# Sixteen blocks instead of ten in the chunked first stage of a retention trunk block, and branch projections with the tokens stationary

## The chip, the cores and the metric

The kernel runs on one core of a Trainium2 chip. The metric is the device time of one execution in microseconds, median of several runs, lower is better. All data is float32. To keep float32 accuracy a matrix product is made of three products of rounded parts: each operand is split into a rounded part ("hi") and the rest ("lo"), and hi·hi, hi·lo and lo·hi are summed.

## The reference, cut to what matters

```python
D_MODEL = 2048; SEQ = 256; RET_HEADS = 8; RET_HEAD_DIM = 256; D_FF = 5632
mod = silu(c) @ w_ada + b_ada                  # 6 vectors of 2048: sh1, sc1, g1, sh2, sc2, g2
xn = rmsnorm(h) * norm1_g * (1 + sc1) + sh1
proj = xn @ w_in                               # 2048 x 18432
q, k, v, g_ret, bg, cg, xc, gate_logits = split(proj)
y_ret = retention(rotary(q), rotary(k), v)     # 8 heads, in 2 chunks of 128 tokens
y_ret = (y_ret * silu(g_ret)) @ w_ret_o
y_conv = (bg * causal_dwconv(cg * xc, w_sc)) @ w_conv_o
gate_a, gate_b = sigmoid(gate_logits + b_gate)
h = h + g1 * ((gate_a * y_ret + gate_b * y_conv) @ w_mix_o)
...
h = h + g2 * (conv_ffn(modulated rmsnorm(h)) )  # w_gate, w_up: 2048 x 5632, w_down
return rmsnorm(h) * final_g
```

## The kernel before, in words

There are 256 tokens, so every weight matrix is streamed once from device memory, 450 MB in all. The work is a list of **units**. A unit is one piece of weights of 256 rows by 512 columns (512 KB). Its `load` (line 288) puts it into a `raw` tile, of which there are six; its `prep` (line 293) has ScalarE write the rounded part (`hi`, line 300) and VectorE the rest (`lo`, line 301); its `run` does the products on TensorE. A loop at line 1023 goes over the list: at step i it calls the load of unit i+9, the preps up to i+4 (first stage) or i+2, and the run of unit i. A tile framework then gives each engine its order of instructions; it may move an instruction forward when a buffer for it is free. SyncE's queue issues all weight loads in one order, and a load waits there until its `raw` slot is free.

Two forms of a unit's products exist. With the **weights stationary** (`w_block`, line 393, result transposed: channels on partitions) a unit is 8 products of 512 columns (hi weights against hi and lo tokens side by side, line 405) and 8 of 256 columns (line 410). With the **tokens stationary** (`x_block` and `start_block`, lines 376 and 454, through `products`, line 367; result has tokens on partitions) a unit is 12 products of 512 columns.

The vector `mod` has its own units (`Ada`, line 306). VectorE multiplies rows of `w_ada` by a scalar and adds them up (lines 335 and 337), and when 2048 rows are through, TensorE turns the sums into columns with a product with ones (`columns_of`, line 351). The stages of the list are:

- **First stage.** xn needs sh1 and sc1, so it becomes ready in chunks of its 16 tiles of 128 channels, `CHUNKS`: 2, 4, 4, 4, 2 tiles. The `Ada` units of chunk n+1 are spread (`spread`, line 539) between the weight units of chunk n, except for the last `TAILS[n+1]` of them. Ten blocks of 512 columns take part: four of v, four of the swish gate, both with the tokens stationary (`start_block`), and q and k of the first pair of heads (`start_turned`, line 498, 24 products of 256 columns a unit). Each block's partial sum of a chunk is copied (chunk 0, ScalarE) or added (later chunks, VectorE, line 465) to a tile; one block (`IN_PSUM`) stays in its accumulator. That makes 80 units.
- **Heads.** q and k of the other three pairs (48 units, weights stationary), rotary, scores, mixing (`retention`). The decay table is loaded once, 1 MB.
- **Branch A.** For each of four column blocks a merge-gate block (`gate_block`, 8 units) and a block of `w_ret_o` (`ret_block`, 8 units), weights stationary: 64 units.
- **Convolution.** 96 units, weights stationary.
- **Branch B.** For each of four column blocks a merge-gate block and a block of `w_conv_o`: 64 units, weights stationary.
- **Mix** (`w_mix_o`, 32 units, tokens stationary), norm, and the gated MLP (176 units with weights stationary, 88 with tokens stationary).

The other 128 `Ada` units (sh2, sc2, g1, g2) are spread over the stages by `ADA_QK, ADA_RET, ADA_CONV, ADA_OUT` = 8, 28, 42, 32, and the rest, 18, over the first 24 units of the mix.

Of the kernel before, what the change touches and what calls it, by code (L numbers as in the profile page):

```python
# [17 lines left out]
P = 128  # L18
# [20 lines left out]
DEFER_SG, DEFER_ROT = (6, 14, 30, 44), 4  # L39
ROT_EARLY = 12  # L40
ADA_QK, ADA_RET, ADA_CONV, ADA_OUT = 8, 28, 42, 32
# [5 lines left out]
def tile_trunk_block(  # L47
# [8 lines left out]
    w_ada, b_ada, w_in, b_gate, w_sc = w_ada[0], b_ada, w_in[0], b_gate[0], w_sc[0]  # L56
# [146 lines left out]
    vec2 = columns([b_gate, w_sc[0], w_sc[1], w_sc[2]], "vec2")  # L203
# [10 lines left out]
    bgate, wsc = vt2[:, 0:32], vt2[:, 32:80]  # L214
# [67 lines left out]
    class Weights:  # L282
        in_big = False

        def __init__(self, w, r0, c0, run):
            self.w, self.r0, self.c0, self.run_ = w, r0, c0, run

        def load(self):
            self.raw = wpool.tile([P, UK, CB], F32, tag="raw", bufs=6, name=nm("raw"))
            src = self.w[self.r0:self.r0 + UK * P, self.c0:self.c0 + CB]  # L290
            nc.sync.dma_start(self.raw, src.rearrange("(k p) n -> p k n", p=P))

        def prep(self):
# [73 lines left out]
    def products(ps, u, xt, k0, t, first, end):  # L367
        for k in range(UK):
# [62 lines left out]
    def xn1_ready(k0, k1):  # L431
        def done(acc):
# [20 lines left out]

    def start_block(j, in_psum):

        dst = [(v_tok, sg_tok)[j // 4][t][:, (j % 4) * CB:(j % 4 + 1) * CB] for t in range(2)]
        st = {}

        def finish(t, ps, n):
            d = dst[t]  # L460
            if n == 0 and not in_psum:
                nc.scalar.copy(d, ps)
                return
            if not in_psum:
                nc.vector.tensor_tensor(d, ps, d, op=ALU.add)
            if n < len(chunks) - 1:
                return
            if j < 4:
                if in_psum:
                    nc.scalar.copy(d, ps)  # L470
            elif in_psum:
                nc.scalar.activation(d, ps, AF.Sigmoid)
                nc.vector.tensor_tensor(d, d, ps, op=ALU.mult)
            else:
                after(DEFER_SG[j - 4], lambda: swish(d))
# [6 lines left out]
        def run_at(n, k0):  # L482
            def run(u):
# [3 lines left out]
                for t in range(2):  # L487
                    ps = st["ps"][t]
                    products(ps, u, xn1_at, k0, t, c0, c1)
                    if k0 + UK == chunks[n][1] and (not in_psum or k0 + UK == KT):  # L490
# [3 lines left out]
        col = (2 + j // 4) * D + (j % 4) * CB  # L494
        return [[Weights(w_in, k0 * P, col, run_at(n, k0)) for k0 in range(*ch, UK)]
                for n, ch in enumerate(chunks)]

    def start_turned(col, done):

        st = {}  # L500

        def run_at(n, k0):
            def run(u):
                c0, c1 = chunks[n]
                if k0 == c0:
                    st["ps"] = [acc_bank() for _ in range(2)]
                if k0 == 0:
                    st["sum"] = w4("sum", [P, 4, S])
                for i in range(4):
                    ps = st["ps"][i // 2][:, (i % 2) * S:(i % 2 + 1) * S]  # L510
                    for k in range(UK):
                        xk = xn1_at(k0 + k)
                        wh, wl = (w[:, k, i * P:(i + 1) * P] for w in (u.hi, u.lo))

                        first = k0 + k == c0 and i % 2 == 0
                        last = k0 + k == c1 - 1 and i % 2 == 1
                        nc.tensor.matmul(ps, lhsT=wh, rhs=xk[:, 0, :], start=first, stop=False)  # L517
                        nc.tensor.matmul(ps, lhsT=wh, rhs=xk[:, 1, :], start=False, stop=False)  # L518
                        nc.tensor.matmul(ps, lhsT=wl, rhs=xk[:, 0, :], start=False, stop=last)  # L519
                    if k0 + UK == c1 and i % 2:  # L520
                        d = st["sum"][:, i - 1:i + 1, :].rearrange("p k s -> p (k s)")
                        if n == 0:
                            nc.scalar.copy(d, st["ps"][i // 2])
                        else:
                            nc.vector.tensor_tensor(d, st["ps"][i // 2], d, op=ALU.add)
                if k0 + UK == KT:
                    after(DEFER_ROT, lambda: done(st["sum"]))
            return run

        return [[Weights(w_in, k0 * P, col, run_at(n, k0)) for k0 in range(*ch, UK)]  # L530
                for n, ch in enumerate(chunks)]
# [26 lines left out]
    for i, u in enumerate([u for u in units if isinstance(u, Weights)]):  # L558
        u.in_big = i % IN_BIG[1] < IN_BIG[0]
# [57 lines left out]
    dec = {}  # L617
# [27 lines left out]
    def retention(pair, st):  # L645

        def scores():
            st["pt"] = []
            for h2 in range(2):
# [15 lines left out]
        def mix():  # L665
            ss = small.tile([P, 4], F32, tag="ss", name=nm("ss"))
            yp = []
            for h2 in range(2):
                pt, hd = st["pt"][h2], 2 * pair + h2
                cols = slice(hd * S, (hd + 1) * S)  # L670
                ps = misc_bank()
                nc.tensor.matmul(ps[:, 0:S], lhsT=pt[:, 0:P], rhs=v_tok[0][:, cols], start=True, stop=True)
                nc.tensor.matmul(ps[:, S:2 * S], lhsT=pt[:, P:S], rhs=v_tok[0][:, cols], start=True, stop=False)
                nc.tensor.matmul(ps[:, S:2 * S], lhsT=pt[:, S:S + P], rhs=v_tok[1][:, cols], start=False, stop=True)
# [5 lines left out]
            for h2 in range(2):  # L680
                hd = 2 * pair + h2
                for t in range(2):
# [3 lines left out]
                        sg_tok[t][:, hd * S:(hd + 1) * S], op0=ALU.mult, op1=ALU.mult,  # L686
# [21 lines left out]
    def load_decay():  # L708
        dec["t"] = blk8("decay", [P, H, S], F32)
# [360 lines left out]
```

## Time and profile before

| | |
|---|---|
| median of 3 runs | 1921.25 us (1920.57 to 1922.83) |
| the profiled execution's own time | 1922.16 us |
| its span, first to last instruction | 1920.3 us |
| TensorE busy | 1872.8 us, 98% |
| VectorE busy | 1366.4 us, 71% |
| ScalarE busy | 904.9 us, 47% |
| read from device memory | 447.03 MB, mean 234 GB/s over the span |

A matmul that is shown as 0.39 us long overlaps with the next one; what counts is the distance from one start to the next. "Idle before" and the name behind the arrow in a row are the wait ahead of the instruction and the operation that ended it.

### The profile page before, as it was taken

The numbers are of one execution on the slowest core, as the hardware profiler recorded it, in microseconds if no ns is written. First come the engines' busy times: TensorE is split into PE (matmuls) and PEld (weight loads), VectorE is DVE, ScalarE is ACT, GpSimd is POOL, SyncE is SP. The second block draws the span as 40 slices with busy tenths as digits, with TensorE's granted clock in tenths as the row PEclk, the third lists the DMA queues.
The fourth block names the chain that finished last, engine by engine and source line by source line (L and its number), as shares of the span: only waits on it lengthen the run. The fifth ranks groups of instructions, "written<-read, shape, count | busy, mean of one in ns | idle before, by whom it ended". The sixth has DMA issues, their size and how long they took to land.

```text
span 1920.3 us, 26558 instructions
## 1 busy us (share of the span) xinstructions
PE 1872.8 (98%) x10151; PEld 1609.6 (84%) x10151; DVE 1366.4 (71%) x1690; ACT 904.9 (47%) x1187; POOL 22.4 (1%) x52
## 2 busy tenths in 40 slices
PE   4999999999999999999999999999999999999998
PEld 3788888888888888888888787888888888888886
DVE  6889987776676777778777786666665456666655
ACT  3544444444444444444445445555554335555543
POOL 1000000000000000000000000000000000000000
PEclk9899999999999999999999999999999999999999
DMA  8989865666878788787888994666665666666653
GB/s 302 322 305 333 290 218 191 192 199 210 271 267 270 260 271 262 255 283 261 272 274 290 315 318 154 186 187 185 194 192 189 195 190 194 187 189 192 209 195 124
DMA packets 220288, 450.88 MB, mean 235 GB/s; under 512 B 14516, under 2 KB 23040, under 8 KB 219648
## 3 DMA queue, kind: packets, MB, share of 16 engines
q1 hardware_dynamic: 218784, 445.84, 70.8%
q10 hardware_dynamic: 864, 3.15, 0.4%
q8 instruction: 79, 1.29, 0.3%
q14 instruction: 49, 0.40, 0.1%
q0 software_dynamic: 512, 0.20, 0.0%
HBM read 447.03 MB, written 2.10 MB: 234 GB/s over the span
## 4 chain that ended last, share of the span: by engine, by line
PE 90%; DVE 4%; DMA 3%; issue 2%; ACT 1%; POOL 0%; SPq 0%; POOLq 0%; DVEq 0%; ACTq 0%
PE acc L405 42%; PE acc L410 21%; PE acc L373 8%; PE acc L374 8%; PE acc L372 8%; DMA raw<-in_w_ada 2%; DVE lo L301 1%; DVE ada L337 1%; PE misc L351 1%; PE acc L519 1%; PE acc L517 1%; PE acc L518 1%; DVE hl L301 0%; PE misc L247 0%; PE misc L653 0%
## 5 line engine op out<-in xcount | busy, mean ns | idle before, releaser
L300 ACT CAST hi<-raw 128x1024 fp32r<-128x1024 f32 x616 | 647.9, 1052 | 831.9 <-PE acc L405 537.6
L301 DVE TENSOR_TENSOR lo<-raw,hi 128x1024 fp32r<-128x1024 f32 x616 | 748.4, 1221 | 354.3 <-ACT hi L300 351.1
L405 PE MATMUL acc<-xn,hi 128*128 128x512 f32 x3072 | 968.6, 397 | 2.9 <-DVE xn L894 1.8
L410 PEld LDWEIGHTS acc<-xn,lo 128*128 128x128 f32 x3072 | 577.8, 188 | 136.6 <-DVE lo L301 0.2
L410 PE MATMUL acc<-xn,lo 128*128 128x256 f32 x3072 | 605.0, 278 | 0.0
L405 PEld LDWEIGHTS acc<-xn,hi 128*128 128x128 f32 x3072 | 468.8, 189 | 5.2 <-DVE xn L894 2.2
L337 DVE SCALAR_TENSOR_TENSOR ada<-raw,c_act,ada 128x1024 f32<-128x1024 f32 (+1 forms) x199 | 238.8, 1200 | 128.0 <-DMA raw<-in_w_ada 127.0
L372 PE MATMUL acc<-hi,ff_t 128*128 128x512 f32 x332 | 129.2, 389 | 0.0
L373 PE MATMUL acc<-lo,ff_t 128*128 128x512 f32 x332 | 129.2, 389 | 0.0
L374 PE MATMUL acc<-hi,ff_t 128*128 128x512 f32 x332 | 129.1, 389 | 0.0
L416 ACT COPY sb<-acc 128x256 f32<-128x256 f32 x224 | 82.5, 368 | 44.9 <-PE acc L410 37.7
L405 PE MATMUL acc<-y_t,hi 128*128 128x512 f32 x256 | 80.5, 396 | 0.0
L405 PE MATMUL acc<-conv_t,hi 128*128 128x512 f32 x256 | 80.4, 395 | 0.0
L374 PEld LDWEIGHTS acc<-hi,ff_t 128*128 128x128 f32 x332 | 62.3, 188 | 13.0
L372 PEld LDWEIGHTS acc<-hi,ff_t 128*128 128x128 f32 x332 | 62.3, 188 | 13.0
L373 PEld LDWEIGHTS acc<-lo,ff_t 128*128 128x128 f32 x332 | 62.3, 188 | 12.7
L373 PE MATMUL acc<-lo,xn 128*128 128x512 f32 x172 | 69.0, 401 | 1.6 <-DVE lo L301 1.5
L372 PE MATMUL acc<-hi,xn 128*128 128x512 f32 x172 | 68.0, 403 | 2.0 <-ACT hi L300 2.0
L374 PE MATMUL acc<-hi,xn 128*128 128x512 f32 x172 | 68.4, 398 | 0.0
L410 PEld LDWEIGHTS acc<-y_t,lo 128*128 128x128 f32 x256 | 47.9, 188 | 13.7 <-DVE lo L301 2.5
L410 PEld LDWEIGHTS acc<-conv_t,lo 128*128 128x128 f32 x256 | 48.0, 188 | 12.9 <-DVE lo L301 1.6
L410 PE MATMUL acc<-y_t,lo 128*128 128x256 f32 x256 | 50.5, 279 | 1.8 <-DVE lo L301 1.8
(204 smaller groups left out, 1619.4 us busy)
## 6 DMA issues: line engine op xcount, KB each, us to landing
raw<-in_w_in SPq DMA_DIRECT2D x288, 512.0 KB, 4.8
raw<-in_w_ada SPq DMA_DIRECT2D x176, 512.0 KB, 4.8
raw<-in_w_gate SPq DMA_DIRECT2D x88, 512.0 KB, 4.4
raw<-in_w_up SPq DMA_DIRECT2D x88, 512.0 KB, 4.4
raw<-in_w_down SPq DMA_DIRECT2D x88, 512.0 KB, 4.4
raw<-in_w_ret_o SPq DMA_DIRECT2D x32, 512.0 KB, 4.7
raw<-in_w_conv_o SPq DMA_DIRECT2D x32, 512.0 KB, 5.4
raw<-in_w_mix_o SPq DMA_DIRECT2D x32, 512.0 KB, 5.6
```

Of the source, the lines that this page charges most:

```text
L300: nc.scalar.copy(self.hi, self.raw)
L301: nc.vector.tensor_tensor(self.lo, self.raw, self.hi.bitcast(F32), op=ALU.subtract)
L337: nc.vector.scalar_tensor_tensor(acc, self.raw[:, k], c_act[:, kt:kt + 1], acc, op0=ALU.mult, op1=ALU.add)
L351: nc.tensor.matmul(ps[:, i:i + 1], lhsT=flat[:, (s0 + i) * P:(s0 + i + 1) * P], rhs=ones[:, 0:1], start=True, stop=True,)
L372: nc.tensor.matmul(ps, lhsT=xh, rhs=u.hi[:, k, :], start=k0 + k == first, stop=False)
L373: nc.tensor.matmul(ps, lhsT=xh, rhs=u.lo[:, k, :], start=False, stop=False)
L374: nc.tensor.matmul(ps, lhsT=xl, rhs=u.hi[:, k, :], start=False, stop=k0 + k == end - 1)
L405: nc.tensor.matmul(ps, lhsT=u.hi[:, k, i * P:(i + 1) * P], rhs=xt(k0 + k).rearrange("p h s -> p (h s)"), start=k0 + k == 0, stop=False,)
L410: nc.tensor.matmul(ps[:, 0:S], lhsT=u.lo[:, k, i * P:(i + 1) * P], rhs=xt(k0 + k)[:, 0, :], start=False, stop=last and k == UK - 1,)
L416: nc.scalar.copy(b, ps[:, S:2 * S])
L517: nc.tensor.matmul(ps, lhsT=wh, rhs=xk[:, 0, :], start=first, stop=False)
L518: nc.tensor.matmul(ps, lhsT=wh, rhs=xk[:, 1, :], start=False, stop=False)
```

## The change

The first stage sums sixteen blocks instead of ten: v, the swish gate and both merge gates (`start_block`, four blocks each), all with the tokens stationary: 128 units' worth of weights. Chunks are now 2, 3, 3, 4, 4 tiles; in a chunk of three tiles a block has one unit of 512 KB and one of half that size (256 KB, `Weights(..., nk)`), and a load of `w_ada` is 384 KB. q and k of the first pair move to the heads' stage, with the weights stationary. The merge gates stay in SBUF as sums; the bias b_gate is loaded broadcast over the partitions (`gate_of`, a `Loaded` unit), added by VectorE, and the sigmoid follows on ScalarE. The decay table is loaded in four parts, one per pair of heads, by the same class. Both kinds of load use the tag `xtmp`, with two buffers.

`ret_block` and `conv_o_block` become `x_block`s: 64 units go from weights stationary to tokens stationary, and the merged result, which now has tokens on partitions, is transposed by TensorE (`turn_mixed`: 8 transposes per column block, 32 in all). The order of the later stages is: heads (q and k of all four pairs, and the first convolution block), branch A (`w_ret_o` alone, 32 units), the rest of the convolution (88 units), branch B (`w_conv_o` alone, 32 units), mix.

```diff
-IN_PSUM = (4,)
-TAILS = (0, 6, 3, 4, 6)
-CHUNKS = [(0, 2), (2, 6), (6, 10), (10, 14), (14, 16)]
-IN_BIG = (1, 3)
+IN_PSUM = (0,)
+TAILS = (0, 3, 4, 4, 4)
+CHUNKS = [(0, 2), (2, 5), (5, 8), (8, 12), (12, 16)]
+IN_WORK = (1, 3)
...
-ADA_QK, ADA_RET, ADA_CONV, ADA_OUT = 8, 28, 42, 32
+ADA_QK, ADA_RET, ADA_CONV, ADA_OUT = 16, 20, 52, 20
...
     class Weights:
...
         def prep(self):
             if self.in_big:
...
+            elif self.in_work:
+                self.hi, self.lo = (
+                    work.tile([P, self.nk, CB], F32R, tag="w4", name=nm(n)) for n in ("hw", "lw"))
...
+    def parts(k0, k1):
+        return [(k, min(UK, k1 - k)) for k in range(k0, k1, UK)]
...
-        dst = [(v_tok, sg_tok)[j // 4][t][:, (j % 4) * CB:(j % 4 + 1) * CB] for t in range(2)]
+        q, c = j // 4, j % 4
+        if q < 2:
+            dst = [(v_tok, sg_tok)[q][c // 2][:, c % 2, t, :] for t in range(2)]
+        else:
+            dst = [(gate_a, gate_b)[q - 2][t][:, c * CB:(c + 1) * CB] for t in range(2)]
...
-    blocks = [start_block(j, j in IN_PSUM) for j in range(8)]
-    ret0 = {}
-    for key in "qk":
-        col = 0 if key == "q" else D
-        blocks.append(start_turned(col, (lambda key: lambda x: rotate(x, ret0, key))(key)))
+    blocks = [start_block(j, j in IN_PSUM) for j in range(16)]
...
+    class Loaded(Call):
...
+        def load(self):
+            self.t = work.tile(self.shape, F32, tag="xtmp", bufs=2, name=nm("ld"))
+            nc.sync.dma_start(self.t, self.src)
...
+    def gate_of(gate, m, j):
+
+        def prep():
+            for t in range(2):
+                g = gate[t][:, j * CB:(j + 1) * CB]
+                nc.vector.tensor_tensor(g, g, got.t, op=ALU.add)
+                nc.scalar.activation(g, g, AF.Sigmoid)
+        c0 = m * D + j * CB
+        got = Loaded(b_gate[0:1, c0:c0 + CB].to_broadcast([P, CB]), [P, CB], prep)
+        return got
+
+    def ret_block(j):
+        cols = slice(j * CB, (j + 1) * CB)
+
+        def e(t, ps):
+            g = gate_a[t][:, cols]
+            nc.vector.tensor_tensor(g, ps, g, op=ALU.mult)
+        return x_block(w_ret_o, 0, j * CB, lambda kt: y_t[kt // 4][:, kt % 4], KT, e)
...
+    def turn_mixed(j):
+        mb = blk8("mixed", [P, 4, 2, S], F32R)
+        mixed.append(mb)
+        for g in range(2):
+            ps = misc_bank()
+            for k in range(2):
+                c0 = (4 * j + 2 * g + k) * P
+                for t in range(2):
+                    nc.tensor.transpose(
+                        ps[:, k * S + t * P:k * S + (t + 1) * P], gate_a[t][:, c0:c0 + P], ident)
+            split(ps.rearrange("p (k s) -> p k s", k=2), mb[:, 2 * g:2 * g + 2])
+
+    def conv_o_block(j):
+        cols = slice(j * CB, (j + 1) * CB)
+
+        def e(t, ps):
+            a, b = gate_a[t][:, cols], gate_b[t][:, cols]
+            nc.vector.tensor_tensor(b, ps, b, op=ALU.mult)
+            nc.vector.tensor_tensor(a, a, b, op=ALU.add)
+            if t == 1:
+                after(2, lambda: turn_mixed(j))
+        return x_block(w_conv_o, 0, j * CB, lambda kt: conv_t[kt // 4][:, kt % 4], KT, e)
```

How this moves instructions shows at three places. In the following rows a name's number is that of its tile; `lo`, `lw` and `hl` are remainders of weights, `ada` the running sum of `w_ada`, `raw` a landed load.

**Chunk 0 on VectorE** (lines 301 and 337 before, 305 and 341 now). Before:

```order
L301 TENSOR_TENSOR lo_335<-raw_299,hi_334 128x1024
L337 SCALAR_TENSOR_TENSOR ada_269<-raw_304,c_act,ada_269 128x1024
L337 SCALAR_TENSOR_TENSOR ada_269<-raw_307,c_act,ada_269 128x1024
L337 SCALAR_TENSOR_TENSOR ada_269<-raw_310,c_act,ada_269 128x1024
L337 SCALAR_TENSOR_TENSOR ada_269<-raw_313,c_act,ada_269 128x1024
L301 TENSOR_TENSOR lo_369<-raw_332,hi_368 128x1024
```

Now:

```order
L305 TENSOR_TENSOR lw_317<-raw_282,hw_316 128x1024
L341 SCALAR_TENSOR_TENSOR ada_272<-raw_286,c_act,ada_272 128x768
L305 TENSOR_TENSOR lo_340<-raw_302,hi_339 128x1024
L341 SCALAR_TENSOR_TENSOR ada_272<-raw_308,c_act,ada_272 128x768
L305 TENSOR_TENSOR lw_349<-raw_311,hw_348 128x1024
```

Four steps of the sum of `w_ada` stood between two units of weights; now there is one, three quarters as wide, and the sixteen steps are spread over thirteen units instead of four.

**One block of chunk 2 on VectorE** (adds are line 465 before, 479 now). Before:

```order
L465 TENSOR_TENSOR v_tok_226<-acc_1147,v_tok_226 128x512
L465 TENSOR_TENSOR v_tok_227<-acc_1148,v_tok_227 128x512
L337 SCALAR_TENSOR_TENSOR ada_968<-raw_1080,c_act,ada_968 128x1024
L301 TENSOR_TENSOR lo_1189<-raw_1112,hi_1188 128x1024
L337 SCALAR_TENSOR_TENSOR ada_968<-raw_1141,c_act,ada_968 128x1024
L301 TENSOR_TENSOR lo_1212<-raw_1161,hi_1211 128x1024
```

Now:

```order
L479 TENSOR_TENSOR v_tok_226<-acc_1433,v_tok_226 128x512
L479 TENSOR_TENSOR v_tok_226<-acc_1434,v_tok_226 128x512
L305 TENSOR_TENSOR lo_1484<-raw_1421,hi_1483 128x512
L305 TENSOR_TENSOR lw_1498<-raw_1427,hw_1497 128x1024
L341 SCALAR_TENSOR_TENSOR ada_1234<-raw_1447,c_act,ada_1234 128x1024
```

A block of chunk 2 was two units of weights and two steps of `ada`; it is now a unit, half a unit and one step, with the same two adds.

**The gate biases, in the heads' stage** (third and fourth pair). SyncE's queue now:

```order
L327 DMA raw_4806<-in_w_ada 128x1024
L681 DMA ld_5301<-in_b_gate 128x512
L292 DMA raw_4828<-in_w_in 128x2x512
L292 DMA raw_4850<-in_w_in 128x2x512
L681 DMA ld_5527<-in_b_gate 128x512
L292 DMA raw_4884<-in_w_in 128x2x512
L681 DMA ld_5696<-in_b_gate 128x512
```

VectorE now:

```order
L305 TENSOR_TENSOR lo_4809<-raw_4607,hi_4808 128x1024
L341 SCALAR_TENSOR_TENSOR ada_3186<-raw_4806,c_act,ada_3186 128x1024
L693 TENSOR_TENSOR gate_a_229<-gate_a_229,ld_5301 128x512
L221 TENSOR_SCALAR r_y_4798<-ss_4781 128x4
L693 TENSOR_TENSOR gate_a_230<-gate_a_230,ld_5301 128x512
L647 SCALAR_TENSOR_TENSOR y_tok_4801<-misc_4782,r_y_4798,sg_tok_228 128x256 x2
L647 SCALAR_TENSOR_TENSOR y_tok_4801<-misc_4790,r_y_4798,sg_tok_228 128x256 x2
L305 TENSOR_TENSOR lo_4831<-raw_4629,hi_4830 128x1024
L693 TENSOR_TENSOR gate_a_229<-gate_a_229,ld_5527 128x512
L693 TENSOR_TENSOR gate_a_230<-gate_a_230,ld_5527 128x512
L305 TENSOR_TENSOR lo_4887<-raw_4692,hi_4886 128x1024
L693 TENSOR_TENSOR gate_a_229<-gate_a_229,ld_5696 128x512
```

VectorE at the same place before, where no gate stood:

```order
L301 TENSOR_TENSOR lo_3490<-raw_3282,hi_3489 128x1024
L301 TENSOR_TENSOR lo_3512<-raw_3304,hi_3511 128x1024
L337 SCALAR_TENSOR_TENSOR ada_2202<-raw_3437,c_act,ada_2202 128x1024
L221 TENSOR_SCALAR r_y_3479<-ss_3462 128x4
L683 SCALAR_TENSOR_TENSOR y_tok_3482<-misc_3463,r_y_3479,sg_tok_228 128x256
```

All eight loads of b_gate, those of branch B included, were moved forward by the framework into the last pairs of heads. Each stands on SyncE's queue between loads of weights, and VectorE's adds of it stand between the remainders of weights. The loads take turns in one of the two `xtmp` buffers, since the fourth pair's decay keeps the other one until its scores are done.

## Rows read from the trace of the kernel before

**Rows 1.** The page: TensorE's busy time, and its granted clock in 40 slices.
```profile
PE 1872.8 (98%) x10151; PEld 1609.6 (84%) x10151; DVE 1366.4 (71%) x1690; ACT 904.9 (47%) x1187; POOL 22.4 (1%) x52
...
PEclk9899999999999999999999999999999999999999
```
**Rows 2.** Timeline of TensorE, weights stationary: start us, us, instruction, count.
```profile
414.61 0.62 PE L405 MATMUL acc<-xn,hi 128*128 128x512 f32 x2
...
439.69 0.63 PE L405 MATMUL acc<-xn,hi 128*128 128x512 f32 x2
```
**Rows 3.** The same timeline, tokens stationary (last down-projection).
```profile
1802.00 0.40 PE L372 MATMUL acc<-hi,ff_t 128*128 128x512 f32 x1
...
1813.11 0.39 PE L373 MATMUL acc<-lo,ff_t 128*128 128x512 f32 x1
```
**Rows 4.** Stretches: us, busy us of PE, PEld, DVE, ACT, POOL, PEclk, DMA share, GB/s.
```profile
32.26:67.11 34.85, 26.64 (x80) 18.65 (x81) 28.54 (x30) 14.57 (x21) 0.00 (x0) 0.71 0.89 312
67.11:280.50 213.39, 212.29 (x1134) 183.51 (x1133) 193.18 (x236) 96.55 (x111) 0.00 (x0) 1.00 0.87 296
...
280.50:437.00 156.50, 156.22 (x898) 136.51 (x897) 117.56 (x149) 69.42 (x105) 3.04 (x3) 1.00 0.60 192
```
**Rows 5.** Timeline of TensorE in chunk 0, waits in brackets.
```profile
32.26 0.93 PE L372 MATMUL acc<-hl,xn 128*128 128x512 f32 x2 [3.29 <-ACT hl L300]
...
39.75 0.50 PE L373 MATMUL acc<-lo,xn 128*128 128x512 f32 x1
...
44.33 0.73 PE L372 MATMUL acc<-hi,xn 128*128 128x512 f32 x2 [2.02 <-ACT hi L300]
...
51.86 0.73 PE L372 MATMUL acc<-hl,xn 128*128 128x512 f32 x2 [1.68 <-ACT hl L300]
...
58.37 2.12 PE L351 MATMUL misc<-ones,ada 128*128 128x1 f32 x16 [1.12 <-DVE ada L337]
...
67.11 0.63 PE L372 MATMUL acc<-hi,xn 128*128 128x512 f32 x2
```
**Rows 6.** Timeline of VectorE in chunk 0.
```profile
45.91 5.24 DVE L337 SCALAR_TENSOR_TENSOR ada<-raw,c_act,ada 128x1024 f32<-128x1024 f32 x4
```
**Rows 7.** Chain of waits: the column products of chunk 2's sums.
```profile
123.39 1.68 PE misc L351 x16
```
**Rows 8.** Timeline of VectorE in chunk 2.
```profile
144.03 1.28 DVE L465 TENSOR_TENSOR v_tok<-acc,v_tok 128x512 f32<-128x512 f32 x2
145.23 1.27 DVE L337 SCALAR_TENSOR_TENSOR ada<-raw,c_act,ada 128x1024 f32<-128x1024 f32 x1
146.43 1.21 DVE L301 TENSOR_TENSOR lo<-raw,hi 128x1024 fp32r<-128x1024 f32 x1
147.56 1.27 DVE L337 SCALAR_TENSOR_TENSOR ada<-raw,c_act,ada 128x1024 f32<-128x1024 f32 x1
```
**Rows 9.** Groups by line: `ada` steps of half width, and the rounding of weights.
```profile
L337 DVE SCALAR_TENSOR_TENSOR ada<-raw,c_act,ada 128x512 f32<-128x512 f32 x30 | 22.4, 745 | 0.3
...
L300 ACT CAST hi<-raw 128x1024 fp32r<-128x1024 f32 x616 | 647.9, 1052 | 831.9 <-PE acc L405 537.6 <-PE acc L374 181.0 <-issue 38.0
```
**Rows 10.** Loads issued from 72 to 230 us: count, KB, median us to landing.
```profile
raw<-in_w_in SPq DMA_DIRECT2D x57, 512.0 KB, 5.0
...
raw<-in_w_ada SPq DMA_DIRECT2D x16, 256.0 KB, 4.4
```
**Rows 11.** The page's DMA issues: reloads of x during the mix.
```profile
h_tok<-in_x SPq DMA_DIRECT2D x8, 256.0 KB, 7.0
```
**Rows 12.** Waits of SyncE's queue, 72 to 280 us: total us, times, longest.
```profile
SPq L291 <- DVE lo L301: 60.4, 36, 4.9
```
**Rows 13.** Timeline of VectorE at the start of branch A.
```profile
475.71 1.28 DVE L337 SCALAR_TENSOR_TENSOR ada<-raw,c_act,ada 128x1024 f32<-128x1024 f32 x1 [5.47 <-DMA raw<-in_w_ada]
```
**Rows 14.** Waits of TensorE after 280.5 us: total us, times, longest.
```profile
PE acc L410 <- DVE lo L301: 3.0, 2, 1.8
```
**Rows 15.** Timeline of TensorE: eight transposes of 128 columns.
```profile
1175.08 1.04 PE L847 MATMUL misc<-ident,h_tok 128*128 128x128 f32 x8
```

More of the change, by code (lines that the diff above doesn't have):

```diff
@@ L367, in products @@
     def products(ps, u, xt, k0, t, first, end):
-        for k in range(UK):
+        for k in range(u.nk):
             xk = xt(k0 + k)
@@ L460, in finish @@
             d = dst[t]
-            if n == 0 and not in_psum:
+            if in_psum or n == 0:
                 nc.scalar.copy(d, ps)
-                return
-            if not in_psum:
+            else:
                 nc.vector.tensor_tensor(d, ps, d, op=ALU.add)
[L466 to L475, printed above, removed]
+            if n == len(chunks) - 1 and q == 1:
+                after(DEFER_SG, lambda: swish(d))
         def swish(d):
@@ L489, in run @@
                     products(ps, u, xn1_at, k0, t, c0, c1)
-                    if k0 + UK == chunks[n][1] and (not in_psum or k0 + UK == KT):
+                    if k0 + nk == c1:
                         finish(t, ps, n)
             return run
-        col = (2 + j // 4) * D + (j % 4) * CB
-        return [[Weights(w_in, k0 * P, col, run_at(n, k0)) for k0 in range(*ch, UK)]
+        col = (2, 3, 7, 8)[q] * D + c * CB
+        return [[Weights(w_in, k0 * P, col, run_at(n, k0, nk), nk) for k0, nk in parts(*ch)]
@@ L496, in start_block @@
                 for n, ch in enumerate(chunks)]
[L498 to L531, printed above, removed]
@@ L706, in retention @@
         return st
-    def load_decay():
-        dec["t"] = blk8("decay", [P, H, S], F32)
-        tc.keep_in_program_order(nc.scalar.dma_start(dec["t"], decay))
-    units.insert(len(units) - 8, Call(load_decay))
-    seq = []
-    for pair in range(4):
-        st = retention(pair, ret0 if pair == 0 else {})
-        if pair > 0:
-            seq += rot_block(pair * CB, st, "q")
-            seq += rot_block(D + pair * CB, st, "k")
-    units += spread(seq, take(ada_mid, ADA_QK))
-    def gate_block(col, store, key):
-        def e(i, a, b):
-            if i == 0:
-                store[key] = w4("gate", [P, 4, S])
-            nc.vector.tensor_tensor(b, a, b, op=ALU.add)
-            t = (col - 7 * D) // P + i
-            nc.scalar.activation(store[key][:, i, :], b, AF.Sigmoid, bias=bgate[:, t:t + 1])
-        return in_block(col, e)
@@ L749, in tile_trunk_block, with __init__, decay_of @@
-    units += spread(seq, take(ada_mid, ADA_RET))
+    class Loaded(Call):
+        def __init__(self, src, shape, prep=None):
+            super().__init__(prep=prep)
+            self.src, self.shape = src, shape
+        def load(self):
+            self.t = work.tile(self.shape, F32, tag="xtmp", bufs=2, name=nm("ld"))
+            nc.sync.dma_start(self.t, self.src)
+    def decay_of(pair, st):
+        got = Loaded(decay[:, 2 * pair:2 * pair + 2, :], [P, 2, S], lambda: st.update(dec=got.t))
+        return got
@@ L783, in e_b @@
                 split(st["y"], yb)
-        return (in_block(5 * D + j * CB, e_c) + in_block(6 * D + j * CB, e_x)
-                + in_block(4 * D + j * CB, e_b))
+        return [in_block(5 * D + j * CB, e_c), in_block(6 * D + j * CB, e_x),
+                in_block(4 * D + j * CB, e_b)]
+    convs = [b for j in range(4) for b in conv_blocks(j)]
+    seq = []
+    for pair in range(4):
+        st = retention(pair, {})
+        seq += rot_block(pair * CB, st, "q")
+        seq.append(decay_of(pair, st))
+        seq += rot_block(D + pair * CB, st, "k")
```

100 lines of the change are left out of this document (40 added, 60 removed).

## The prediction, made before the changed kernel was run

> **What bounds the kernel now.** I read the page first. TensorE is busy 98% of the span [rows 1], but its instructions overlap, so I went to the timeline for the distance from start to start. With the weights stationary, 36 groups of two 512-column and two 256-column products take 25.08 us [rows 2], 0.697 us each; four groups make a unit, 2.787 us. With the tokens stationary, 49 steps take 11.11 us [rows 3], 0.2267 us each; twelve make a unit, 2.720 us. The list has 448 units of the first form after 280.5 us and 120 of the second: 448 x 2.787 + 120 x 2.720 = 1575.0 of the 1639.8 us that are left there. The other 64.8 us are retention, transposes, broadcasts, the second norm and the tail, which the change leaves. So from 280.5 us on TensorE sets the time, and almost nothing is to be had there except by a cheaper form.
>
> Then I split the first stage [rows 4]. From 67.11 to 280.5 us TensorE runs through: 59 units with tokens stationary are 160.5 us, 48 column products at 0.105 [rows 7] are 5.0, and what is left, 47.9, is at most 2.99 for each of the 16 turned units. From the first weight product at 32.26 to 67.11 us it is different: five units, 13.6 us of work, take 34.85. The rows of TensorE show waits for weights of 2.02 and 1.68 us between units [rows 5], and VectorE shows why: between two units it does four `ada` steps, 5.24 us [rows 6], and the next unit's remainder comes after them. The waits also cost the clock: its mean over this stretch is 0.71 [rows 4], between its two levels of 1.2 and 2.4 GHz. The fourteen products from 32.26 to 39.75 us take 0.53 us each; the ten from there to the wait that ends at 44.33 take 0.26, near the full pace; the twelve after this wait, up to the next one, again 0.49 [rows 5]. The clock rose after TensorE had worked on and fell after it had waited 2 us. About 21 us are lost here, and this is the largest loss that the change can touch.
>
> **The change, part by part.** All sums are against the profiled execution: span 1920.3, time 1922.2, so 1.9 us lie around the span; the median of the runs is 0.9 us below it.
>
> *Chunk 0.* Sixteen units now stand against sixteen `ada` steps of three quarters the width, thirteen of the units mixed with them. Per unit VectorE has one remainder, 1.13 us by its distance to the next instruction, and 16/13 of a step. A step of 384 columns twice is not in the trace; it lies between 0.745 [rows 9] and 1.20 us [rows 8], and I take 0.95, the middle of the two, hence 2.3 us a unit, under TensorE's 2.72. Loads: 0.524 MB and 16/13 of 0.393 MB, 1.01 MB a unit; at the 312 GB/s of this stretch [rows 4], which contains times when the queue had nothing to issue, 3.2 us; over thirteen units that could hold TensorE back by some 2.5 us, and it is part of the waits taken below. At first TensorE is slower than either (5.1 us a unit at the low clock), so a stock of units builds up, it does not wait, and the clock rises as it did at 39.75. Up to there 14 products took 7.49 us instead of 3.17: a loss of 4.3, and the only one that I take. The first product itself stays at 32.26 us: the first chunk of `ada` is as wide as before.
>
> *First stage as a whole.* 32.26 + 4.3 + 128 x 2.720 (348.2) + 56 column products x 0.105 (5.9) = 390.7 us. VectorE must keep up. A block of chunk 2 was two remainders, two adds and two steps, 2 x 1.13 + 1.20 + 2 x 1.20 = 5.86 us [rows 8], against 5.44 of TensorE. A block is now a remainder and half a one (1.13 + 0.60, the half priced as one of the two adds, which have its size), two adds 1.20, one step 0.95 (chunk 1) or 1.20 (chunk 2): 3.88 or 4.13 us against 18 x 0.2267 = 4.08. In chunk 3 it is 1.13 x 2 + 1.20 + 1.20 = 4.66 against 5.44. So VectorE is just enough, with a lead of about one block. I take 3 us of waits; the lower end is 0, the upper 25 (second rival). End of the stage: 393.7.
>
> *The rest.* Of the 448 units, the 64 of the gates went into the first stage and 64 of the branches changed form; the 16 of q and k came in: 336 x 2.787 + 184 x 2.720 = 936.4 + 500.5 us. The branches' change of form alone is 64 x 0.067 = 4.3 us. The Trainium skill (TensorE: Matmul & The Clock Gate, Back-to-back issue gap) gives another price: a gap of N/2.4 + 2.5 ns, by which I estimate 2.59 us for the one form and 2.60 for the other, and the 4.3 us would be nothing; rows 2 and 3, from one execution, differ by 0.067 us, and I go by them. The other work is 64.8 us as before. The 32 added transposes are 0.13 us each by eight in 1.04 [rows 15]: 4.2. Their copies replace the split of the merged result. The four decay loads replace one, and each is issued well before its scores: nothing, unless they queue with the gate biases, which the next part prices.
>
> *The gate biases.* Eight loads of 256 KB pass through one buffer, each issued only after VectorE's adds of the one before, and each holds VectorE, in order, until it lands. Landing is 4.4 us by the nearest row [rows 10], 7.0 in a crowded stretch [rows 11]. By the order of rows VectorE has 1.1 to 8 us of other work between one bias's adds and the next's; for five or six of the eight it is short by 1 to 3 us, about 11 together. The adds are 8 x 1.20 = 9.6. VectorE is idle 39 of 156.5 us in the heads' stage [rows 4], 12 in the 50 us concerned, so it falls behind by 8 to 9. A wait of 5.47 us on VectorE [rows 13] left TensorE no longer wait than 1.8 anywhere later [rows 14]: the stock of two prepared units covers some 5. I take 4; the ends are 0 and 20 (landing 7.0).
>
> *Crowding.* Twenty `ada` steps instead of 18 in the mix, 52 loads in 32 units of branch A and of B: 2 us, from the 1.8 us waits of [rows 14]; the lower end is 0.
>
> Sum: 393.7 + 936.4 + 500.5 + 64.8 + 4.2 + 4 + 2 = 1905.6; with the 1.9 around it 1907.5, against the median 1906.6. I say **1907**. The gain of 14 us is the 17 us of chunk 0's waits and clock, some 9 of cheaper form, less 4 of transposes and 7 to 9 of new waits.
>
> **The rivals.** *Gate biases at full price*: the loads land late behind the weights of the same queue, and VectorE's hold is paid by TensorE: 6 to 16 us on top, 1913 to 1923. For it: eight holds in a row on one buffer; against: landing 4.4 us and the cover above.
>
> *Raw slots* (the one on the slower side): six `raw` slots now carry smaller loads. SyncE's queue does wait for VectorE to free a slot, 36 times for a remainder alone [rows 12]. A block of chunks 1 and 2 needs three loads; at TensorE's pace 4.08 us each slot must turn round in 8.2 us. Landing 5.0, cast 1.05 [rows 9] and remainder 1.13 make 7.2; in [rows 8] a slot turned in 5.86 x 6/4 = 8.8 with VectorE never idle; over all of chunk 1, 39 loads (23 of weights, 16 of `w_ada`) in the 65 us from 58.37 [rows 5] to 123.39 [rows 7], it was 10.0. At 10.0 a block takes 5.0 us, 0.92 more, 29 for the 32 blocks, less a lead of 4: 1929. It decides from about 8.5 us a turn on, where the lead is used up; at 9.5 nothing of the gain is left. The Trainium skill (DMA: Bandwidth & Descriptors, Bandwidth) speaks for it: loads should be batched to a megabyte or more, small ones paying a fixed cost of about 2 us; no row gives that cost, and [rows 10] has 256 KB landing sooner than 512.
>
> *The clock falls again in chunk 0*: three gaps, each 4.3 us: 1920, no change.
>
> *The form is worth nothing*: the distance of 0.2267 us holds where one `raw` unit after the other is ready, and in the branches, beside the `ada` steps, the 128 units that change form stay at 2.787. That is 8.6 us more, 1916. The Trainium skill's gap, above, comes to the same; rows 2 and 3 speak against it.
>
> **How the numbers follow.** A measurement of this kernel can tell a difference of about 0.2%, 3.8 us. Forecast (1900 to 1912) 0.58; everything hidden, all three waits 0 and the clock rising sooner, 1896 to 1899, 0.05; gate biases 0.15, of it 0.08 below 1917.4; raw slots 0.11, of it 0.10 slower; clock 0.08, of it 0.06 no change and 0.02 slower; form 0.03. Faster is 0.58 + 0.05 + 0.08 + 0.03 = 0.74, no change 0.07 + 0.01 + 0.06 = 0.14, slower 0.10 + 0.02 = 0.12. The range goes from 1896 to 1925: it leaves out the upper part of the raw slots.
>
> **What would show it.** Chunk 0 without waits of TensorE over 1 us and a clock mean near 0.9 between 32 and 67 us; the first product of 512 columns with weights stationary at 391 to 397 us; blocks of chunks 1 and 2 at 4.1 to 4.3 us; steps of 0.227 us in branches A and B; the heads' stage with waits for `ld` on VectorE and under 6 us on TensorE. Wrong it is if the first stage ends after 405 us, or if TensorE waits over 10 us in the third and fourth pair of heads.

## The result, and the profile after

The changed kernel is slower: 1947.8 us (median of 4 runs, 1940.5 to 1949.7) against 1921.0 before, a ratio of 1.0131 with a 95% interval of 1.0104 to 1.0157 (four runs of each). The forecast was 1907, its range ended at 1925. The profiled execution took 1947.83 us, its span is 1945.9.

The page of the changed kernel: busy times, and the chain of waits by engine.

```profile
PE 1880.9 (97%) x9543; PEld 1583.9 (81%) x9543; DVE 1385.3 (71%) x1695; ACT 892.2 (46%) x1150; POOL 22.0 (1%) x51
...
PE 75%; DMA 12%; DVE 8%; issue 3%; ACT 1%; POOL 0%; SPq 0%; DVEq 0%; POOLq 0%; ACTq 0%
PE acc L409 26%; PE acc L414 13%; DMA raw<-in_w_ada 12%; PE acc L377 11%; PE acc L376 11%; PE acc L378 11%; DVE lo L305 4%; DVE ada L341 2%; PE misc L355 1%; DMA ld<-in_b_gate 0%; PE misc L247 0%; PE misc L619 0%; ACT hi L304 0%; DVE gate_b L783 0%; DMA raw<-in_w_in 0%
```

Busy shares have hardly moved [rows 1]. New is that 12% of the chain are landings of `w_ada`, which were 2% in the kernel before: TensorE no longer sets the time everywhere. The stages, cut at the first product of each kind on TensorE (first stage, heads, branch A, rest of the convolution, branch B, mix), with the columns of [rows 4]:

```profile
32.26:67.11 34.85, 32.66 (x126) 25.24 (x127) 24.84 (x24) 20.42 (x30) 0.00 (x0) 0.92 0.89 293
67.11:399.60 332.49, 331.69 (x1471) 271.32 (x1470) 285.92 (x358) 152.33 (x184) 0.00 (x0) 1.00 0.81 269
399.60:638.20 238.60, 231.41 (x1314) 200.44 (x1313) 170.71 (x215) 105.84 (x163) 4.41 (x5) 0.99 0.65 205
638.20:736.90 98.70, 92.92 (x403) 74.56 (x402) 65.14 (x63) 34.04 (x33) 0.00 (x0) 0.98 0.80 262
736.90:1000.10 263.20, 255.55 (x1445) 220.35 (x1444) 206.20 (x248) 117.75 (x153) 4.70 (x9) 0.99 0.84 279
1000.10:1103.30 103.20, 95.55 (x414) 74.55 (x413) 77.12 (x80) 39.18 (x42) 1.44 (x2) 1.00 0.81 272
```

Chunk 0 does what was forecast: TensorE is busy 32.66 of 34.85 us where it was 26.64, the clock's mean is 0.92 where it was 0.71, and after the wait for the very first product none up to 67.11 us is longer than the 0.5 us of these two:

```profile
32.46 0.80 PE L376 MATMUL acc<-hi,xn 128*128 128x512 f32 x1 [2.35 <-ACT xn L92]
...
49.63 0.73 PE L376 MATMUL acc<-hi,xn 128*128 128x512 f32 x2 [0.48 <-ACT hi L304]
...
50.89 0.50 PE L377 MATMUL acc<-lo,xn 128*128 128x512 f32 x1 [0.53 <-DVE lo L305]
```

The first stage ends at 399.6 us, 5.9 after the sum's 393.7. The greater loss comes behind it. By the sum's own rates, without the column products, branch A is 32 x 2.720 = 87.0 us and took 98.7; the 88 units of the convolution are 245.3 and took 263.2; branch B with its transposes is 91.2 and took 103.2. VectorE's waits in these three stages, one fence for each:

```profile
DVE ada L341 <- DMA raw<-in_w_ada: 33.5, 17, 3.8
DVE ada L339 <- DMA raw<-in_w_ada: 1.0, 1, 1.0
```

```profile
DVE ada L341 <- DMA raw<-in_w_ada: 50.7, 37, 3.7
DVE lo L305 <- ACT hi L304: 4.4, 7, 1.2
```

```profile
DVE ada L341 <- DMA raw<-in_w_ada: 26.0, 15, 4.5
DVE lo L305 <- ACT hi L304: 0.2, 1, 0.2
```

Add VectorE's busy time to these. Branch A: 65.1 + 33.5 + 1.0 = 99.6 of 98.7 us (an instruction at either edge counts in full). Branch B: 77.1 + 26.2 = 103.3 of 103.2. Convolution: 206.2 + 50.7 + 4.4 = 261.3 of 263.2. VectorE, 71% busy by the page, is full there: what it does not work, it stands waiting for loads of `w_ada`. A wait of `lo` for `hi` is the opposite sign: VectorE is ahead, and the next `hi` comes when TensorE has used up an older one. Of these waits it has next to none left.

Why it waits shows on VectorE and on SyncE's queue, in branch A:

```profile
660.61 1.29 DVE L341 SCALAR_TENSOR_TENSOR ada<-raw,c_act,ada 128x1024 f32<-128x1024 f32 x1 [1.75 <-DMA raw<-in_w_ada]
661.81 2.36 DVE L305 TENSOR_TENSOR lo<-raw,hi 128x1024 fp32r<-128x1024 f32 x2
...
666.56 1.28 DVE L341 SCALAR_TENSOR_TENSOR ada<-raw,c_act,ada 128x1024 f32<-128x1024 f32 x1 [1.20 <-DMA raw<-in_w_ada]
667.76 2.35 DVE L305 TENSOR_TENSOR lo<-raw,hi 128x1024 fp32r<-128x1024 f32 x2
672.83 1.29 DVE L341 SCALAR_TENSOR_TENSOR ada<-raw,c_act,ada 128x1024 f32<-128x1024 f32 x1 [2.71 <-DMA raw<-in_w_ada]
```

```profile
654.76 0.37 SPq L292 DMA_DIRECT2D raw<-in_w_ret_o  x1
...
661.92 0.34 SPq L327 DMA_DIRECT2D raw<-in_w_ada  x1
...
667.88 0.34 SPq L327 DMA_DIRECT2D raw<-in_w_ada  x1
```

The load issued at 661.92, right after the step that ended at 661.9 gave its slot back, is used at 666.56, the moment it lands; the next is issued at 667.88, right after that step, and used at 672.83. And the order of VectorE's rows (each name ends in two numbers, the first of which rises in the order of the loads) puts these steps ahead of weights that were loaded before them:

```order
L341 SCALAR_TENSOR_TENSOR ada_1087_5186<-raw_1155_5548,c_act_102,ada_1087_5186 128x1024
L305 TENSOR_TENSOR lo_1160_5569<-raw_1141_5470,hi_1159_5568 128x1024
L305 TENSOR_TENSOR lo_1164_5592<-raw_1147_5494,hi_1163_5591 128x1024
...
L341 SCALAR_TENSOR_TENSOR ada_1087_5186<-raw_1162_5589,c_act_102,ada_1087_5186 128x1024
L305 TENSOR_TENSOR lo_1171_5633<-raw_1154_5533,hi_1170_5632 128x1024
```

`raw_1154`, issued at 654.76, is in SBUF and rounded by 665.5; its remainder waits until 667.76 behind the step of `raw_1162`, issued seven microseconds later. In branch A a step overtakes 3.1 weights in the mean. The queue of the loads closes the circle: from 638.2 to 736.9 us SyncE itself stands waiting for landings of `w_ada` before it can issue the next load, of `w_ada` or of weights, 27.3 us in 16 waits:

```profile
SPq L327 <- DMA raw<-in_w_ada: 15.5, 9, 3.1
...
SPq L292 <- DMA raw<-in_w_ada: 11.8, 7, 3.6
```

That VectorE's queue is strictly first in, first out is also what the Trainium skill states (PSUM — Partial Sum Buffer, Engine vs sequencer instructions), and this case's rows agree: a remainder whose data lay ready stood still.

### The profile page after: what moved, and what is told of

Its sections match the earlier page's. It is cut to its first block, busy times and chain, and to the rows that moved or that the text cites. A ratio compares the mean times of both kernels' runs of the same rounds, so it can differ in the third digit from the quotient of the medians.

```text
span 1945.9 us, 25399 instructions
## 1 busy us (share of the span) xinstructions
PE 1880.9 (97%) x9543; PEld 1583.9 (81%) x9543; DVE 1385.3 (71%) x1695; ACT 892.2 (46%) x1150; POOL 22.0 (1%) x51
## 4 chain that ended last, share of the span: by engine, by line
PE 75%; DMA 12%; DVE 8%; issue 3%; ACT 1%; POOL 0%; SPq 0%; DVEq 0%; POOLq 0%; ACTq 0%
PE acc L409 26%; PE acc L414 13%; DMA raw<-in_w_ada 12%; PE acc L377 11%; PE acc L376 11%; PE acc L378 11%; DVE lo L305 4%; DVE ada L341 2%; PE misc L355 1%; DMA ld<-in_b_gate 0%; PE misc L247 0%; PE misc L619 0%; ACT hi L304 0%; DVE gate_b L783 0%; DMA raw<-in_w_in 0%
## 5 line engine op out<-in xcount | busy, mean ns | idle before, releaser
L304 ACT CAST hi<-raw 128x1024 fp32r<-128x1024 f32 (+1 forms) x601 | 623.4, 1038 | 837.8 <-PE acc L409 394.9
L305 DVE TENSOR_TENSOR lo<-raw,hi 128x1024 fp32r<-128x1024 f32 (+1 forms) x601 | 720.5, 1204 | 343.5 <-ACT hi L304 341.6
L409 PE MATMUL acc<-xn,hi 128*128 128x512 f32 x2688 | 852.3, 398 | 11.3 <-DVE qk L606 5.5
L414 PEld LDWEIGHTS acc<-xn,lo 128*128 128x128 f32 x2688 | 507.2, 189 | 128.3 <-DVE lo L305 9.6
L414 PE MATMUL acc<-xn,lo 128*128 128x256 f32 x2688 | 532.4, 280 | 5.1 <-DVE lo L305 4.9
L341 DVE SCALAR_TENSOR_TENSOR ada<-raw,c_act,ada 128x1024 f32<-128x1024 f32 (+2 forms) x199 | 239.0, 1201 | 121.0 <-DMA raw<-in_w_ada 120.3
L376 PE MATMUL acc<-hi,xn 128*128 128x512 f32 x304 | 119.5, 397 | 4.1 <-ACT xn L92 2.3
L378 PE MATMUL acc<-hi,xn 128*128 128x512 f32 x304 | 119.5, 394 | 0.0
L378 PE MATMUL acc<-hw,xn 128*128 128x512 f32 x208 | 82.0, 394 | 0.0
L377 PE MATMUL acc<-lw,xn 128*128 128x512 f32 x208 | 81.9, 394 | 0.0
L376 PE MATMUL acc<-hw,xn 128*128 128x512 f32 x208 | 81.3, 395 | 0.0
L376 PEld LDWEIGHTS acc<-hi,xn 128*128 128x128 f32 x304 | 57.5, 190 | 17.7 <-ACT xn L92 2.4
```

What stands on the lines that cost most here:

```text
L341: nc.vector.scalar_tensor_tensor(acc, self.raw[:, k], c_act[:, kt:kt + 1], acc, op0=ALU.mult, op1=ALU.add)
L376: nc.tensor.matmul(ps, lhsT=xh, rhs=u.hi[:, k, :], start=k0 + k == first, stop=False)
L377: nc.tensor.matmul(ps, lhsT=xh, rhs=u.lo[:, k, :], start=False, stop=False)
L378: nc.tensor.matmul(ps, lhsT=xl, rhs=u.hi[:, k, :], start=False, stop=k0 + k == end - 1)
L409: nc.tensor.matmul(ps, lhsT=u.hi[:, k, i * P:(i + 1) * P], rhs=xt(k0 + k).rearrange("p h s -> p (h s)"), start=k0 + k == 0, stop=False,)
L414: nc.tensor.matmul(ps[:, 0:S], lhsT=u.lo[:, k, i * P:(i + 1) * P], rhs=xt(k0 + k)[:, 0, :], start=False, stop=last and k == UK - 1,)
```

## The experiments

**Theory 1** is this hold: each `ada` step keeps VectorE until its own load lands, and branches and convolution have become too dense for it. **Theory 2** is that the heads, 238.6 us, lose by the gate biases. The **rival** is that the branches lose by their new form. `tc.keep_in_program_order`, in the edits below, keeps the framework from moving an instruction out of the order in which the program writes it.

### 1. Steps spread evenly

```diff
-ADA_QK, ADA_RET, ADA_CONV, ADA_OUT = 16, 20, 52, 20
+ADA_QK, ADA_RET, ADA_CONV, ADA_OUT = 38, 14, 44, 14
```

> The changed kernel with its ada steps spread more evenly: 38 in the heads, 14 in branch A, 44 in the rest of the convolution, 14 in branch B, 18 in the mix (it had 16, 20, 52, 20, 20). By time at TensorE's pace that is one step every 5.8, 6.2, 5.6, 6.2 us in the first four stages, where it was 13.8, 4.4, 4.7, 4.4. Theory 1 (each ada step holds VectorE until its own load lands, 4.7 us after the step before gave the slot back, so that about 5 us a step is the least): branch A takes 88 to 91 us (was 100.6), branch B 90 to 93 (was 103), the convolution 252 to 256 (was 261), the heads 239 to 244, together 1920 to 1927 us. Rival (the branches lose by their new form, by its two accumulators and the copies that follow): branch A stays at 98 to 101 us, B at 101 to 103, the whole 1943 to 1950.

Measured: 1939.4 us (ratio 1.0087, 1.0059 to 1.0116), over the range of theory 1 and under that of the rival. The convolution came to 252.3 as forecast and branch B to 93.9, just over its range; the heads rose to 245.9, over theirs, and branch A stayed at 97.8 with 14 steps. There VectorE still waited:

```profile
DVE ada L341 <- DMA raw<-in_w_ada: 33.4, 12, 5.9
```

Density alone, one step in 5 us, is therefore not the whole cause: at one in 7 us branch A lost as much.

### 2. Gate biases kept in place

```diff
-            nc.sync.dma_start(self.t, self.src)
+            tc.keep_in_program_order(nc.sync.dma_start(self.t, self.src))
```

> The changed kernel with the loads of the gate biases and decays kept where the program writes them: one bias in each block of branch A and of branch B, none in the heads. Theory 2 (eight biases through one buffer hold VectorE and SyncE's queue in the last pairs of heads): the heads take 224 to 231 us (were 238.8), branches A and B stay within 3 us of 100.6 and 103, the whole 1933 to 1942. If the heads lose their 16 to 18 us by something else (the retention itself, more work between their units than before): heads 236 to 240, the whole 1945 to 1951.

1935.2 us (ratio 1.0057, 1.0035 to 1.0078): the heads took 229.9 instead of 238.6, branches A and B 95.0 and 102.6. VectorE's waits for `ld`, 12.3 us in the heads of the changed kernel, are gone from them. Theory 2 holds, at 8.7 us. That branch A fell by 3.7 us was not forecast; VectorE's waits for `w_ada` fell there from 34.5 to 26.0 us.

### 3. Later ada steps in load order

```diff
-                nc.vector.scalar_tensor_tensor(
+                step = nc.vector.scalar_tensor_tensor(
                     acc, self.raw[:, k], c_act[:, kt:kt + 1], acc, op0=ALU.mult, op1=ALU.add
                 )
+                if self.c1 - self.c0 == CB:
+                    tc.keep_in_program_order(step)
```

> The changed kernel with only the order on VectorE of the 128 later ada steps changed: each stands in the order of the program, which is the order in which SyncE issues the loads, where it stood ahead of the remainders of up to four weights that had been loaded before it. Number and places of the loads stay. Theory 1 in its form 'order' (VectorE stands still for a load that is still on its way while weights that have landed wait behind): branch A 88 to 92 us, B 90 to 94, convolution 252 to 257, the whole 1918 to 1928. In its form 'too many loads' (20 steps with six slots cannot be served in 87 us in any order): branch A over 97, the whole 1940 to 1950. Rival by the branches' form: the same as that.

1912.7 us, 35 less than the changed kernel, 5 under the forecast range, and faster than the kernel before (ratio 0.9943, 0.9922 to 0.9964). Only the place of the steps on VectorE was prescribed. The order of the loads on SyncE stayed, but for 29 of 901 places around the loads of the biases, of the decay and of x; which `raw` slot a load takes follows from the order, and changed with it. VectorE's waits from 399 us to the end of the mix, of the changed kernel and then of this one:

```profile
DVE ada L341 <- DMA raw<-in_w_ada: 118.7, 79, 4.5
DVE lo L305 <- ACT hi L304: 54.2, 53, 2.9
```

```profile
DVE lo L305 <- ACT hi L304: 132.8, 138, 2.9
...
DVE ada L339 <- DMA raw<-in_w_ada: 3.8, 3, 2.4
```

The 118.7 us are gone and have become room, waits for TensorE's pace. SyncE's own waits for landings of `w_ada`, 100.8 us (75 times) in the same stretch of the changed kernel, are down to 4.2 (3 times). The stages of this kernel, branch A to B:

```profile
632.90:727.00 94.10, 92.55 (x403) 76.59 (x402) 67.07 (x64) 34.07 (x33) 0.00 (x0) 0.96 0.85 285
727.00:979.30 252.30, 252.27 (x1446) 219.32 (x1445) 206.69 (x250) 117.86 (x152) 4.70 (x9) 0.99 0.87 290
979.30:1070.90 91.60, 91.60 (x414) 75.22 (x413) 76.38 (x79) 39.15 (x42) 1.44 (x2) 1.00 0.89 308
```

Convolution and branch B are as forecast, and the same loads now come at 290 and 308 GB/s where they came at 279 and 272, so it was neither their number nor the queue. The branches' form is the same as in the changed kernel, so the rival falls. Branch A is 2 us above its range: TensorE waits 1.5 us there for the last step of a group before the column products, and the clock's mean is 0.96. The order of the steps and the slots that follow from it were changed as one; no run tells them apart.

### 4. The first two edits together

The edits of 1 and 2.

> The first and the second edit together. Theories 1 and 2 both right: heads 226 to 232 us, branch A 88 to 92, convolution 252 to 256, branch B 90 to 94, the whole 1906 to 1916, under the kernel before. Only theory 1: 1920 to 1927. Only theory 2: 1933 to 1942. Neither: 1943 to 1950.

1937.9 us (ratio 1.0077, 1.0050 to 1.0103): a miss. The whole fits "only theory 2", the stages do not: the heads took 242.7, branch A 95.4, branch B 99.1. As long as steps stand ahead of weights, moving loads about moves the holds about; the savings of 1 and 2 did not add up.

### 5. Load order and gate biases in place

The edits of 2 and 3.

> The edits of the second and third experiment together: gate biases in place, later ada steps in load order. In the third the heads took 233.9 us, in the second 229.9. If the two costs are separate, the heads take 227 to 231 us, branch A 90 to 95, branch B 90 to 93, the whole 1904 to 1911, some 4 us under the third. If the biases cost only where the ada steps were out of order, the whole stays at 1910 to 1915.

1914.1 us (ratio 0.9950, 0.9937 to 0.9963): no gain over the third, in the range forecast for that case. The heads fell by 6.0 to 227.9, and branch B rose by 5.7 to 97.4, where VectorE now waits for biases, 7.2 us beside 82.3 us of work in 97.4. A hold costs where VectorE has no room.

### 6. Load order and even spread

The edits of 1 and 3.

> Load order (as in the third experiment) and the even spread of the first together. If the order alone is the cause, the density of the steps no longer matters: the whole stays within 4 us of the third experiment's 1912.7, branch A 90 to 95 us, branch B 89 to 93. If twenty steps in 87 us still cost something in load order, branches A and B fall by 3 to 5 us together and the whole to 1903 to 1908.

1904.1 us (ratio 0.9891, 0.9874 to 0.9908), the fastest that computes the whole block, under both kernels. So density still cost something in load order: of these 8.6 us 4.8 are in branch A, where column products had waited, the rest comes in pieces of under 2 us, against a first stage that was 3.7 us longer in the profiled execution. TensorE from the heads to the mix:

```profile
402.80:635.00 232.20, 229.91 (x1330) 200.78 (x1329) 191.68 (x235) 104.30 (x157) 4.72 (x5) 1.00 0.77 254
635.00:724.30 89.30, 89.30 (x403) 73.94 (x402) 62.86 (x62) 36.72 (x39) 1.53 (x2) 1.00 0.82 277
724.30:974.90 250.60, 250.60 (x1433) 217.29 (x1432) 198.90 (x242) 118.90 (x155) 4.60 (x9) 1.00 0.83 278
974.90:1064.70 89.80, 89.80 (x411) 74.59 (x410) 69.21 (x72) 37.95 (x40) 0.00 (x0) 1.00 0.82 275
```

Clock 1.00 throughout, no wait in the branches. This is how the prediction had the branches run.

### 7. The kernel before, with its steps in load order

The edit of 3 in the kernel before.

> The kernel before with only its later ada steps put into load order. If the old spacing, one step in 5.6 to 6.4 us from the heads to branch B, gave each load the time it needed (TensorE's waits from 399 us to the end of the mix are 6 us together), the time falls by 0 to 5 us, 1917 to 1923. If the old kernel paid for the same order as well, hidden in the 64.8 us that the prediction put down to other work, it falls by more than 8 us, under 1914, and the change's own part of the gain of the third experiment is less than it seemed.

1918.3 us (ratio 0.9970, 0.9961 to 0.9979), about 6 us or 0.3%, a little more than the 0 to 5 that were expected. The old kernel had the same order (a step overtook 2.5 to 3.8 weights from the heads to branch B), and its VectorE waited no less. From 280.3 us to the end of its mix:

```profile
DVE ada L337 <- DMA raw<-in_w_ada: 126.8, 83, 5.5
DVE lo L301 <- ACT hi L300: 80.8, 82, 2.4
```

In load order 2.9 us of these waits for `w_ada` are left. The old kernel could afford them. Its branch B, with a step every 5.5 us, had 119.4 us of work and 33.9 of these waits in 159.3:

```profile
920.30:1079.60 159.30, 158.11 (x903) 136.89 (x901) 119.36 (x137) 78.23 (x106) 1.45 (x2) 1.00 0.84 280
...
DVE ada L337 <- DMA raw<-in_w_ada: 33.9, 23, 3.3
```

So the change did not bring the holds; it took the room that covered them. With both kernels in load order the change itself is worth 5.6 us (1918.3 to 1912.7), and with its steps spread evenly 14.2.

### 8 and 9. The price of the gate biases

The sixth kernel with the edit of 2; and the sixth without the biases, which leaves out the eight loads of `b_gate` and the sixteen adds, so that the gates are the sigmoid of the sums alone.

> The sixth experiment with the gate biases also kept in place, one in each block of branch A and of branch B. In load order the biases in place took 6.0 us off the heads and put 5.7 us on branch B, where VectorE had no room. With the even spread branch B has 14 ada steps instead of 20: if VectorE's room decides, the heads take 225 to 229 us (232.2 in the sixth), branch B 90 to 92 (89.8), the whole 1897 to 1903. If a bias costs the same wherever it stands, the whole stays within 3 us of the sixth's 1904.1.

> The sixth experiment without the gate biases: the eight loads of b_gate and the sixteen adds are left out, the gates are the sigmoid of the sums alone. This is the price of the term 'gate biases' by itself, which the prediction put at 4 us (0 to 20). At 4 us the heads take 228 us and the whole 1900; at the 6 to 9 us that the second and fifth experiment showed in the heads, 223 to 226 and 1895 to 1898; if the rest of the heads' time is the retention, nothing changes, 1902 to 1906.

1905.1 us (ratio 0.9918, 0.9886 to 0.9951) and 1901.7 (0.9894, 0.9868 to 0.9919). The heads took 231.8 us in both, 232.2 in the sixth. What came true is the branch of each forecast in which little changes: the eighth is within 3 us of the sixth, and the ninth has the heads unchanged and ends 0.3 us under its 1902. Once the steps stand in order and are spread, the medians put all the biases at 2.4 us where the framework moves them (sixth against ninth) and at 3.4 in place (eighth against ninth), about what these runs can tell. In place they no longer cost the heads anything but put 2.5 us on branch B, 92.3 instead of 89.8. What is left of the heads' time is TensorE's own work, busy 229.91 of 232.20 us in the row above.

## Why the prediction was wrong, step by step

**What bounds the kernel.** That "from 280.5 us on TensorE sets the time" was right for the old kernel and the wrong question for the new one. I read TensorE's waits there (3.0, 2 times [rows 14]) and a single 5.47 us wait of VectorE [rows 13], and noted that it left TensorE no wait over 1.8. I did not add up that wait's group: 126.8 us, 83 times, which in branch B left VectorE 6.0 of 159.3 us (seventh experiment).

**Crowding, 2 us: the step that failed.** It was priced by what late steps had cost TensorE before, 1.8 us, where it had to be priced by what a step costs VectorE, and compared with VectorE's room. What the runs showed in its place: 118.7 us of waits on VectorE from the heads to the mix, and 35 us of time that load order alone took back (third experiment). The rows were there. From 461.8 to 1079.6 us of the kernel before:

```profile
DVE ada L337 <- DMA raw<-in_w_ada: 111.7, 71, 5.5
...
DVE ada L335 <- DMA raw<-in_w_ada: 5.4, 3, 3.7
```

That is 117.1 us for the 99 steps of this stretch, 1.18 each, beside the 1.20 of the step itself. With VectorE's work in the new stages and 18, 52 and 21 steps that fall into them, branch A comes to 65.1 + 21.2 = 86.3 us, the convolution to 206.2 + 61.4 = 267.6, branch B to 77.1 + 24.8 = 101.9. TensorE needs 89.3, 250.6 and 89.8 (sixth experiment): the larger of the two, worked out afterwards and with VectorE's work as measured, gives +17 and +12 where +13 and +13 were measured. Branch A does not come out so: by this price VectorE had room, but its 18 waits are 1.9 us each, and it took 9 us more than the sixth experiment's. There SyncE's waits for landings of `w_ada`, 27.3 us, are the densest too. Why a step waits longer there, and 2.6 us in 13 waits of the first experiment, was not tried and stays open; that the waits go with the order is shown for it as well.

**The gate biases, 4 us (0 to 20).** Mis-sized by half: 8.7 us in the second experiment, 6.0 in the fifth, about 3 once VectorE had room. The mechanism was right, and so was the bound; "TensorE waits over 10 us in the third and fourth pair of heads" did not come true.

**Chunk 0 and the first stage.** Right in the mechanism. No wait over 1 us, clock 0.92. A step of 384 columns twice, taken as 0.95 us, is 0.93 from start to start. The stage ends 5.9 us late. Up to 67.11 us 6.3 are lost instead of 4.3 (126 products in 34.85 us instead of 126 x 0.2267 = 28.6), but not by the clock: it was low only to about 38.4 us (mean 0.52 from the first product), where 14 products took 5.95 us, 2.8 too many, and it stayed at 1.00 through the waits that followed. Four waits at the start of units, 1.9 us together, and wider gaps beside them make most of the rest. The 4.3 had itself held a wait of 1.18 us for `hl`, put down to the clock. From 67.11 us on TensorE waits 0.8 us in all, but the products stand about 0.231 us apart instead of 0.2267, some 6 us over the stage; why is open.

**The rates.** Right from the heads on. With room on VectorE the branches run 226 products in 51.23 us, 0.2267 each (sixth experiment, first and last of the row):

```profile
636.14 0.39 PE L380 MATMUL acc<-hi,y_t 128*128 128x512 f32 x1
...
687.37 0.39 PE L378 MATMUL acc<-hi,y_t 128*128 128x512 f32 x1
```

The rival "the form is worth nothing" is not borne out. Nor are, for these two forms, the equal times that I had estimated from the gap in the Trainium skill (TensorE: Matmul & The Clock Gate, Back-to-back issue gap), which the page gives for an isolated product.

**The rival on the slower side.** It named the slots of `raw`, in chunks 1 and 2. There TensorE hardly waited. In the branches the slots did turn late, but because a step waiting on VectorE held them, not by the size of the loads: in load order the same loads passed. The time of 1929 was too short and for another reason.

**The sum.** The forecast sum, 1905.6 us of span, lies close to the 1903.2 of the sixth experiment, but this is luck in part. There the first stage ended 9.1 us later than in the sum, at 402.8, and everything behind it took 1500.4 us instead of 1511.9: the work beside the 520 units, 75.0 in the sum, was 63.5. With a VectorE that keeps up, the later stages thus stay under the sum; no term of it asked whether VectorE does keep up.

## What to carry to other kernels

An engine's room is its stage less its busy time less its own waits for loads; before making a stage faster or denser, add up these waits for the second engine too, per step, even where the first engine shows none. Where a scheduler sets the order, compare the order of use with the order of loads: a consumer placed ahead of data that came earlier makes that data wait for its own landing, here 1.2 to 1.9 us a step in the mean. Pinning it took back 35 us here, and bought 6 in a kernel that seemed to have nothing to gain.

## What the runs showed that was not expected

From the heads to the end of the mix the changed kernel is 44.6 us longer than the sixth (399.6 to 1196.9 us against 402.8 to 1155.5), but the waits that the trace names on TensorE there are only 29.5 us together:

```profile
PE acc L377 <- DVE lo L305: 11.1, 12, 2.3
PE acc L409 <- DVE qk L606: 5.5, 2, 3.4
PE acc L414 <- DVE lo L305: 4.9, 6, 1.4
PE acc L409 <- DVE sb L722: 4.1, 3, 2.3
PE misc L774 <- DVE gate_a L784: 2.8, 7, 1.1
PE misc L828 <- DVE h_tok L815: 1.1, 2, 0.9
```

In branch A the same products are busy 92.92 us instead of 89.30, at a mean clock of 0.98 instead of 1.00; in branch B 95.55 instead of 89.80 with the clock at 1.00 in both. The list of named waits was here a lower bound of what a late supplier cost.
